# Storing some heads in pairs, with one input buffer and four output buffers, in a QK^T kernel on one core

## The chip, the core and the metric

The kernel runs on one core of a Trainium2 chip. The metric is the device time of one execution in microseconds (us); a verdict compares medians of several executions. Before the change the median of 3 runs is 1062.53 us (1062.45 to 1062.65).

A core has a matrix engine (PE) that writes to PSUM, a vector engine (DVE), a scalar engine (ACT), a GpSimd engine (POOL) and a sync engine (SP). SP and ACT issue DMA transfers here; the transfers themselves are carried out by 16 DMA engines that move data between HBM (the arrays in_q, in_k, out) and SBUF (the kernel's tiles).

## The reference

```python
def setup_inputs():
    batch, n_heads, seq, head_dim = 8, 12, 1024, 64
    ...
def reference(q, k):
    return np.einsum('bhid,bhjd->bhij', q, k).astype(np.float32)
```

There are 96 heads. For each, a 1024 x 64 matrix q is multiplied by the transpose of a 1024 x 64 matrix k, and the 1024 x 1024 float32 product is written out. Inputs are 2 x 25 MB, the output is 403 MB: 4 MB for a head.

## The kernel before

**Blocks.** The heads are taken in blocks of 2, 2, 4, 8, 8 and six times 12 (`sizes`, line 77). A block's q and k are loaded, cast to float16, and transposed so that the 64 columns lie on the partitions, before its first head can be multiplied. Blocks 0 and 1 are transposed by PE (`transpose_rows`, line 238). All later ones go through POOL, which casts 32-partition pieces into one of two half buffers (`cast_quads`, line 201, the cast on line 211), and DVE, which transposes 32 x 32 squares of a half buffer into qT or kT (`transpose_quads`, line 222, line 230). A block's q is cast and transposed in two parts, then its k in two parts (`chunks`, line 193; `CHUNK`, line 80, would cut them finer).

**One head.** `scores` (line 256) takes a head in four steps (index u, from head 1 on): PE multiplies two 128-row pieces of q with all of k into one half of PSUM (line 312), and ACT copies that half to an output buffer in SBUF (line 289, 128 x 2048 elements). When all four copies are done, SP issues one DMA that stores the head (line 302).

**Buffers.** There are three output buffers (`o_sb`, line 94), taken in a ring: the copies of a head wait until the store of the head three before it has landed (`out_free`). At the start the first output buffer holds the inputs of blocks 0 to 2 (lines 330 to 343). There are two input buffers (`x_sb`, line 88), in a ring too, one for q and one for k.

**What sets the order.** Every engine works through its own list in the order in which the Python code appends to it; semaphores alone tie the lists together. `run` and `wait` (lines 29 and 33) put a wait in front of an instruction, and nothing behind a waiting instruction on its engine goes ahead. DMA issues are entries of SP's or ACT's list.

**Loads.** The early loads and block 3's two loads are issued at the very start; store 0 also waits until block 3's q has landed (line 300). The rest form a `stream` (line 344): q and k of block 4, of block 5, and so on. `next_load` (line 350) issues the next one on ACT. `block` (line 391) calls it after the copy of step u = 1 of certain heads: heads 1 and 3 of block 2, heads 4 and 6 of blocks 3 and 4, and heads 6 and 8 of the 12-head blocks (`LOADS`, line 81; line 410). DVE's transposes for the next block, and POOL's casts, are appended along the heads of a block (lines 407 to 413).

Of the kernel before, what the change touches and what calls it, by code (L numbers as in the profile page):

```python
# [7 lines left out]
F32 = mybir.dt.float32  # L8
P = 128
# [50 lines left out]
def kernel(  # L60
# [6 lines left out]
    nc = tc.nc  # L67

    B, H, S, D = q.shape
    NT = S // P  # L70
    BH = B * H
# [2 lines left out]
    flat = [x.rearrange("b h s d -> (b h s) d") for x in (q, k)]  # L74
    of = out.rearrange("b h i j -> (b h) i j")

    sizes = [2, 2, 4, 8, 8] + [12] * ((BH - 24) // 12)
    PE_BLOCKS, EARLY = 2, 3
    NMAX = max(sizes)
    CHUNK, HALVES = 96 * 32, 2  # L80
    LOADS = {0: (), 1: (), 2: (1, 3), 3: (4, 6), 4: (4, 6)}

    pool = ctx.enter_context(tc.tile_pool(name="sb", bufs=1))
    psum = ctx.enter_context(
        tc.tile_pool(name="ps", bufs=1, space=bass.MemoryType.PSUM)
    )
    ident = pool.tile([P, P], F16, tag="ident")
    x_sb = [pool.tile([P, NMAX * S * D // P], F32, name=f"x_sb{i}", tag=f"x{i}") for i in range(2)]
    half_sb = [pool.tile([P, CHUNK], F16, name=f"half{i}", tag=f"half{i}") for i in range(HALVES)]
    qk_sb = [  # L90
        [pool.tile([P, NMAX * S // 2], F16, name=f"{'qk'[x]}T{i}") for x in range(2)]
        for i in range(2)
    ]
    o_sb = [pool.tile([P, NT, S], F32, name=f"o_sb{i}", tag=f"out{i}") for i in range(3)]
    ps_all = psum.tile([P, 4 * S], F32, tag="po")

    ctx.enter_context(tc.tile_critical())  # L97
# [2 lines left out]
    act = Engine(nc, nc.scalar, "act_done")  # L100
    dve = Engine(nc, nc.vector, "dve_done")
    gps = Engine(nc, nc.gpsimd, "pool_done")
    sp = Engine(nc, nc.sync, "sp_done")
# [18 lines left out]
    n, at = S * D // P * 2, 8 * S // 2  # L122
# [5 lines left out]
            for h in range(2)  # L128
        ]
    )  # L130
    inputs = Ring(x_sb)
    outs = Ring(o_sb)
    input_landing = {id(t): Landing(nc, f"x{i}_in") for i, t in enumerate(x_sb)}
    store_landing = {id(t): Landing(nc, f"out{i}_out") for i, t in enumerate(o_sb)}

    class Block:
        def __init__(self, i, first, N):
            self.i, self.first, self.N = i, first, N
            self.by_pe = i < PE_BLOCKS
            self.R = N * S // P  # L140
            self.elems = self.R * D
            self.cut = max(1, -(-self.R * 32 // CHUNK))
            self.raw = [None] * 2
            self.landed = [[] for _ in range(2)]
            self.raw_busy = [None] * 2
            self.rows = [None] * 2
            self.halves = {}
            self.qk = qk_sb[i % 2]
            self.ready = []
            self.over = []  # L150

        def load(self, x, eng, landing=None):
            events = []
            if self.raw[x] is None:
                buf, events, self.raw_busy[x] = inputs.next()
                self.raw[x] = buf[:, : self.elems]
                landing = input_landing[id(buf)]
            src = flat[x][self.first * S : (self.first + self.N) * S]
            eng.wait(events)
            dma = eng.eng.dma_start(  # L160
                out=self.raw[x], in_=src.rearrange("(p r) d -> p (r d)", p=P)
            )
            self.landed[x].append(landing.start(dma))
# [10 lines left out]
        def cast_rows(self, x):  # L174
            n = S * D // P
            buf, events, busy = rooms.next()
            rows = buf[:, : 2 * n].rearrange("p (r h d) -> p r h d", h=2, d=D)
            for h in range(2):
                done = gps.run(
                    lambda: nc.gpsimd.tensor_copy(  # L180
                        out=rows[:, :, h],
                        in_=self.raw[x][:, h * n : (h + 1) * n].rearrange(
                            "p (r d) -> p r d", d=D
                        ),
                    ),
                    events + [self.landed[x][h]],
                )
            self.rows[x] = rows, done, busy
            if self.raw_busy[x] is not None:
                self.raw_busy[x].append(done)  # L190
            return done

        def chunks(self):
# [7 lines left out]
        def cast_quads(self, x, part, c):  # L201
            m = self.R // self.cut
            buf, events, busy = (rooms if self.i == PE_BLOCKS else halves).next()
            dst = buf[:, : m * 32]
            raw = self.raw[x].rearrange("p (r h d) -> p r h d", h=2, d=32)
            for half in range(2):
                b = 2 * half + part
                for h in range(2):
                    q0 = 32 * (2 * half + h)
                    done = gps.run(  # L210
                        lambda: nc.gpsimd.tensor_copy(  # L211
                            out=dst[q0 : q0 + 32].rearrange("p (r d) -> p r d", d=32),
                            in_=raw[32 * b : 32 * b + 32, c * m : (c + 1) * m, h],
                        ),
                        events + self.landed[x],
                    )
            self.halves[x, part, c] = dst, done, busy
            if self.raw_busy[x] is not None:
                self.raw_busy[x][:] = [done]
            return done  # L220

        def transpose_quads(self, x, part, c):
# [33 lines left out]
        def scores(self, n, side, regions, w):  # L256
            half, g = divmod(n, self.N // 2)
            cs = slice(half * D, (half + 1) * D)
            qT = self.qk[0].rearrange("c (g m t) -> c g t m", t=NT, m=P)
            kT = self.qk[1].rearrange("c (g j) -> c g j", j=S)  # L260
            buf, out_free, out_busy = outs.next()
            written = {}
            for u in range(NT // w):
                ps, ps_free, ps_busy = regions.next()
                first = True
                for tt in range(w):
                    stationary = qT[cs, g, w * u + tt]
                    done = pe.run(
                        lambda: load_weights(stationary, half * D),
                        self.ready if n == 0 and u == 0 else [],  # L270
                        signal=False,
                    )
                    for j in range(2):
                        at = tt * S + j * 512
                        done = pe.run(
                            lambda: multiply(
                                ps[:, at : at + 512],
                                stationary,
                                kT[cs, g, j * 512 : (j + 1) * 512],
                                half * D,  # L280
                            ),
                            ps_free,
                            signal=tt == w - 1 and j == 1,
                        )
                dst = buf[:, w * u : w * u + w].rearrange("p t j -> p (t j)")
                by_dve = w == 1 and u % 2
                copier = dve if by_dve else act
                copied = copier.run(
                    lambda: (nc.vector.tensor_copy if by_dve else nc.scalar.copy)(  # L289
                        out=dst, in_=ps[:, : w * S]  # L290
                    ),
                    out_free + [done],
                )
                written[copier] = copied
                ps_busy.append(copied)
                for do in side.get(u, []):
                    do()
            self.over = [done]
            sp.wait(written.values())
            if self.first + n == 0:  # L300
                sp.wait(blocks[EARLY].landed[0])
            dma = nc.sync.dma_start(
                out=of[self.first + n].rearrange("(p t) j -> p (t j)", p=P),
                in_=buf.rearrange("p t j -> p (t j)"),
            )
            out_busy.append(store_landing[id(buf)].start(dma))

    def load_weights(stationary, at):
        return nc.tensor.ldweights(stationary, tile_position=(at, 0))  # L309
# [18 lines left out]
        first += N  # L328

    early, _, early_busy = outs.next()  # L330
    raw = early.rearrange("p t j -> p (t j)")
    at = 0
    for b in blocks[:EARLY]:
        for x in range(2):
# [15 lines left out]
    def next_load(eng):  # L350
        if stream:
            b, x = stream.pop(0)
            assert b.i == EARLY or not any(i == b.i - 1 and c[0] == x for i, c in casts)
            b.load(x, eng)

    for x in range(2):
# [34 lines left out]
    def block(i, heads, regions, w):  # L391
        b = blocks[i]
        nxt = blocks[i + 1] if i + 1 < len(blocks) else None
        for n in heads:
# [10 lines left out]
                    }  # L405
            elif nxt:
                parts = nxt.chunks()
                some = [s for m, s in enumerate(parts) if m * b.N // len(parts) == n]
                side = {0: [lambda s=s: transposed(nxt, s) for s in some]}
            if n in LOADS.get(i, (6, 8)):  # L410
                side[1] = side.get(1, []) + [lambda: next_load(act)]
            b.scores(n, side, regions, w)
            to_half(i + 2 + (n == b.N - 1))

# [15 lines left out]
    block(0, [1], halves_ps, 2)  # L430
    for i in range(1, len(blocks)):
        block(i, range(blocks[i].N), halves_ps, 2)
    sp.wait([(c, c.count) for c in store_landing.values()])


# [28 lines left out]
```

## Time and profile before

| | |
|---|---|
| median of 3 runs | 1062.53 us |
| span of the profiled execution, first to last instruction | 1060.4 us |
| PE, ACT, DVE, POOL busy | 66%, 66%, 44%, 33% of the span |
| moved by DMA | 453.19 MB: 50.33 MB read from HBM, 402.65 MB written to it |
| mean rate over the span | 427 GB/s |
| one ACT copy of 128 x 2048 | 1.86 us, four for a head |
| one head's store, issue to landing | 21.7 us (median), 4096 KB |
| one 12-head load, issue to landing | 22.0 us (median), 3072 KB |
| one transpose of 128 x 3072 by DVE, one cast of 32 x 3072 by POOL | 14.2 us, 2.5 us |
| granted TensorE clock | 1.000 |

The profiled execution is one of its own; it is not among the three that were timed. Its span leaves out what lies before the first and after the last instruction. Times of single instructions and transfers are counted from the start of the span. In the profile, q1 is the queue of the DMAs that SP issues and q10 that of those from ACT. An engine's idle time is put down to what ended it; an idle engine that nothing waits for costs nothing.

### The profile page before, as it was taken

The page shows a single profiled execution, that of the slowest core. Times are in us where ns is not written, and L with a number is a line of the kernel's source. Part 1 is how long each engine was busy: PE and PEld are TensorE (multiplying, and loading weights), DVE is VectorE, ACT ScalarE, POOL GpSimd, SP SyncE. Part 2 cuts the span into 40 slices and gives each one's busy share as a digit, 9 for nine tenths or more (in the row PEclk, how much of TensorE's full clock was granted, in tenths as well). Part 3 has the DMA queues.
Part 4 walks back from the last instruction along what each step waited for, and adds up shares of the span by engine and source line. Part 5 has one row for each costly group of instructions (what it writes and reads, how often), then busy time and mean ns, then how long its engine had stood idle before and what let it go on. Part 6 is the DMA issues. An engine that isn't in the chain of part 4 may idle for free.

```text
span 1060.4 us, 3258 instructions
## 1 busy us (share of the span) xinstructions
PE 700.5 (66%) x1568; PEld 127.3 (12%) x800; DVE 470.6 (44%) x43; ACT 697.0 (66%) x386; POOL 345.3 (33%) x158
## 2 busy tenths in 40 slices
PE   6876755765577557774577855777557777778770
PEld 2111100110111001110011100111001111111110
DVE  2998602991795006960069600795007950000000
ACT  4766755755678557775577755776557777777771
POOL 7667216436360430704307053160531600000000
DMA  9999999999999999999999999999999999999997
GB/s 376 434 435 434 432 419 430 435 428 431 433 432 428 428 435 430 430 431 423 438 431 429 433 431 434 434 429 422 426 432 435 429 434 434 434 435 430 431 434 336
DMA packets 17583, 453.19 MB, mean 427 GB/s; under 512 B 1952, under 2 KB 1952, under 8 KB 2976
## 3 DMA queue, kind: packets, MB, share of 16 engines
q1 hardware_dynamic: 14976, 410.00, 90.0%
q10 hardware_dynamic: 2592, 42.99, 9.7%
q8 instruction: 9, 0.15, 0.0%
q14 instruction: 6, 0.05, 0.0%
HBM read 50.33 MB, written 402.65 MB: 427 GB/s over the span
## 4 chain that ended last, share of the span: by engine, by line
DMA 71%; ACT 17%; PE 7%; DVE 2%; issue 1%; POOL 0%; ACTq 0%; SPq 0%
DMA out_dram<-o_sb 70%; ACT o_sb L289 17%; PE ps_all L312 7%; DVE kT L230 1%; DVE qT L230 1%; DMA o_sb<-in_q_dram 0%; PE ps_all L244 0%; POOL qT L180 0%; DVE kT L251 0%; ACT kT L251 0%; ACTq L36 0%; SPq L168 0%; SPq L459 0%; SPq L97 0%
## 5 line engine op out<-in xcount | busy, mean ns | idle before, releaser
L289 ACT COPY o_sb<-ps_all 128x2048 f32<-128x2048 f32 (+1 forms) x384 | 694.7, 1859 | 333.0 <-DMA out_dram<-o_sb 301.6
L312 PE MATMUL ps_all<-kT,qT 64*128 64x512 f16 x1536 | 696.4, 617 | 327.8 <-ACT o_sb L289 322.4
L211 POOL CAST half<-x_sb 32x3072 f16<-32x3072 f32 (+1 forms) x128 | 323.4, 2527 | 491.6 <-DMA x_sb<-in_q_dram 242.2
L230 DVE STREAM_TRANSPOSE qT<-half 128x3072 f16<-128x3072 f16 (+1 forms) x16 | 222.9, 14132 | 370.0 <-PE ps_all L312 370.0
L309 PEld LDWEIGHTS <-qT 64*128 64x128 f16 x768 | 124.2, 162 | 896.8 <-issue 889.2
L230 DVE STREAM_TRANSPOSE kT<-half 128x3072 f16<-128x3072 f16 (+1 forms) x16 | 224.2, 14217 | 2.8 <-POOL half L211 2.8
L230 DVE STREAM_TRANSPOSE kT<-kT 128x1024 f16<-128x1024 f16 x2 | 9.3, 4836 | 0.0
L230 DVE STREAM_TRANSPOSE qT<-qT 128x1024 f16<-128x1024 f16 x2 | 9.2, 4784 | 0.0
L211 POOL CAST qT<-o_sb 32x1024 f16<-32x1024 f32 x8 | 8.3, 1034 | 1.2 <-DMA o_sb<-in_q_dram 0.8
L211 POOL CAST kT<-o_sb 32x1024 f16<-32x1024 f32 x8 | 8.3, 1033 | 0.5
L251 DVE COPY qT<-ps_all 128x1024 f16<-128x1024 f16 x2 | 2.5, 1225 | 11.0 <-PE ps_all L244 11.0
L289 DVE COPY o_sb<-ps_all 128x1024 f32<-128x1024 f32 x4 | 4.9, 1225 | 4.4 <-PE ps_all L312 4.4
L244 PE MATMUL ps_all<-ident,qT 128*128 128x128 f16 x16 | 2.1, 310 | 6.7 <-POOL qT L180 6.6
L251 ACT COPY kT<-ps_all 128x1024 f16<-128x1024 f16 x1 | 1.0, 1012 | 4.7 <-PE ps_all L244 4.7
L180 POOL CAST qT<-o_sb 128x512 f16<-128x512 f32 x4 | 2.3, 612 | 3.6 <-DMA o_sb<-in_q_dram 3.6
L251 DVE COPY kT<-ps_all 128x1024 f16<-128x1024 f16 x1 | 1.2, 1225 | 4.4 <-PE ps_all L244 4.4
L251 ACT ACT_TABLE_LOAD x1 | 1.3, 1283 | 2.8 <-issue 2.8
L244 PE MATMUL ps_all<-ident,kT 128*128 128x128 f16 x16 | 2.0, 305 | 0.7 <-ACT o_sb L289 0.7
L180 POOL CAST kT<-o_sb 128x512 f16<-128x512 f32 x4 | 2.3, 613 | 0.4 <-DMA o_sb<-in_q_dram 0.4
L244 PEld LDWEIGHTS ps_all<-ident,qT 128*128 128x128 f16 x16 | 1.5, 140 | 6.9 <-POOL qT L180 6.9
L244 PEld LDWEIGHTS ps_all<-ident,kT 128*128 128x128 f16 x16 | 1.5, 136 | 3.3 <-POOL qT L211 1.6
L359 POOL MEMSET ident<- 128x128 f16 x1 | 0.2, 205 | 0.5 <-SPq L97 0.5
(5 smaller groups left out, 0.7 us busy)
## 6 DMA issues: line engine op xcount, KB each, us to landing
out_dram<-o_sb SPq DMA_DIRECT2D x96, 4096.0 KB, 21.7
x_sb<-in_q_dram ACTq DMA_DIRECT2D x6, 3072.0 KB, 22.0
x_sb<-in_k_dram ACTq DMA_DIRECT2D x6, 3072.0 KB, 21.9
x_sb<-in_q_dram SPq DMA_DIRECT2D x1, 2048.0 KB, 14.6
x_sb<-in_k_dram SPq DMA_DIRECT2D x1, 2048.0 KB, 19.6
x_sb<-in_q_dram ACTq DMA_DIRECT2D x1, 2048.0 KB, 18.3
x_sb<-in_k_dram ACTq DMA_DIRECT2D x1, 2048.0 KB, 19.1
o_sb<-in_k_dram ACTq DMA_DIRECT2D x4, 256.0 KB, 4.7
```

The lines of the kernel that those rows point to most:

```text
L180: lambda: nc.gpsimd.tensor_copy(out=rows[:, :, h], in_=self.raw[x][:, h * n : (h + 1) * n].rearrange("p (r d) -> p r d", d=D),),
L211: lambda: nc.gpsimd.tensor_copy(out=dst[q0 : q0 + 32].rearrange("p (r d) -> p r d", d=32), in_=raw[32 * b : 32 * b + 32, c * m : (c + 1) * ...
L230: lambda: nc.vector.transpose(out=dst, in_=buf.rearrange("p (r i) -> p r i", i=32)),
L244: lambda: nc.tensor.transpose(t_ps[:, t], rows[:, t], ident),
L251: lambda: copy(out=dst, in_=t_ps.rearrange("c t m -> c m t")), [done]
L289: lambda: (nc.vector.tensor_copy if by_dve else nc.scalar.copy)(out=dst, in_=ps[:, : w * S]),
L309: return nc.tensor.ldweights(stationary, tile_position=(at, 0))
L312: return nc.tensor.add_instruction(mybir.InstMatmult(name=nc.get_next_instruction_name(), ins=[nc.tensor.lower_ap(moving), nc.tensor.lower ...
L359: cleared = gps.run(lambda: nc.gpsimd.memset(ident, 0.0))
```

## The change

- A head whose number is in `PAIRS` isn't stored by itself: it is held, and the next head's store takes both in one DMA of 8 MB, out of two output buffers that lie side by side. `PAIRS` holds the third head before each load, so the pair is made of the heads 3 and 2 before the one at which a load is issued.
- A load is issued at the first step of the heads in `LOADS` (6, 10, 14, 19, then every sixth head from 24 to 78), ahead of that head's first copy, behind a wait for the landing of the store that frees its output buffer, that is of the head four before it.
- Four output buffers, all in one tile; one input buffer for q and k in turn (block 3's two lie side by side in it). A load waits for the last cast of the load before it, of whichever of q and k.
- Blocks of 2, 2, 4, 6, 10 and six times 12. Casts and transposes are cut in half (`CHUNK`): 48 rows of 32 instead of 96. `TURNS` tells at which heads they are appended.

```diff
-    sizes = [2, 2, 4, 8, 8] + [12] * ((BH - 24) // 12)
+    sizes = [2, 2, 4, 6, 10] + [12] * ((BH - 24) // 12)
...
-    CHUNK, HALVES = 96 * 32, 2
-    LOADS = {0: (), 1: (), 2: (1, 3), 3: (4, 6), 4: (4, 6)}
+    CHUNK, HALVES, OUTS = 48 * 32, 2, 4
+    TURNS = {6: (0, 0, 1, 2, 3, 3, 4, 5), 10: (1, 2, 3, 4, 6, 7, 8, 9), 12: (2, 3, 4, 5, 8, 9, 10, 11)}
+    LOADS = [6, 10, 14, 19] + [m for h in range(24, BH - 12, 12) for m in (h, h + 6)]
+    PAIRS = {m - 3 for m in LOADS}
...
-    x_sb = [pool.tile([P, NMAX * S * D // P], F32, name=f"x_sb{i}", tag=f"x{i}") for i in range(2)]
+    x_sb = pool.tile([P, NMAX * S * D // P], F32, name="x_sb", tag="x")
...
-    o_sb = [pool.tile([P, NT, S], F32, name=f"o_sb{i}", tag=f"out{i}") for i in range(3)]
+    o_sb = pool.tile([P, OUTS, NT * S], F32, name="o_sb", tag="out")
...
-    inputs = Ring(x_sb)
-    outs = Ring(o_sb)
+    input_busy = []
+    outs = Ring(list(range(OUTS)))
...
+    held = []
...
         def load(self, x, eng, landing=None):
             events = []
             if self.raw[x] is None:
-                buf, events, self.raw_busy[x] = inputs.next()
-                self.raw[x] = buf[:, : self.elems]
-                landing = input_landing[id(buf)]
+                at = x * self.elems if self.i == EARLY else 0
+                self.raw[x] = x_sb[:, at : at + self.elems]
+                landing = input_landing[x]
+                events = list(input_busy)
...
         def cast_quads(self, x, part, c):
...
-            if self.raw_busy[x] is not None:
-                self.raw_busy[x][:] = [done]
+            if self.i >= EARLY:
+                input_busy[:] = [done]
...
         def scores(self, n, side, regions, w):
...
-            buf, out_free, out_busy = outs.next()
+            i, out_free, out_busy = outs.next()
+            head = self.first + n
...
-                dst = buf[:, w * u : w * u + w].rearrange("p t j -> p (t j)")
+                dst = o_sb[:, i, w * u * S : w * (u + 1) * S]
+                if u == 0 and head in LOADS:
+                    act.wait(out_free)
+                    next_load(act)
...
+            held.append((i, out_busy))
+            if head in PAIRS:
+                return
             sp.wait(written.values())
-            if self.first + n == 0:
+            if head == 0:
                 sp.wait(blocks[EARLY].landed[0])
+            i, N = held[0][0], len(held)
             dma = nc.sync.dma_start(
-                out=of[self.first + n].rearrange("(p t) j -> p (t j)", p=P),
-                in_=buf.rearrange("p t j -> p (t j)"),
-            )
-            out_busy.append(store_landing[id(buf)].start(dma))
+                out=of[head - N + 1 : head + 1].rearrange("h (p t) j -> p h (t j)", p=P),
+                in_=o_sb[:, i : i + N],
+            )
+            stored = store_landing[i].start(dma)
+            for _, busy in held:
+                busy.append(stored)
+            held.clear()
...
-                some = [s for m, s in enumerate(parts) if m * b.N // len(parts) == n]
+                at = TURNS.get(b.N) or [m * b.N // len(parts) for m in range(len(parts))]
+                some = [s for m, s in zip(at, parts) if m == n]
                 side = {0: [lambda s=s: transposed(nxt, s) for s in some]}
-            if n in LOADS.get(i, (6, 8)):
-                side[1] = side.get(1, []) + [lambda: next_load(act)]
```

More of the change, by code (lines that the diff above doesn't have):

```diff
@@ L130 @@
     )
-    inputs = Ring(x_sb)
-    outs = Ring(o_sb)
-    input_landing = {id(t): Landing(nc, f"x{i}_in") for i, t in enumerate(x_sb)}
-    store_landing = {id(t): Landing(nc, f"out{i}_out") for i, t in enumerate(o_sb)}
+    input_busy = []
+    outs = Ring(list(range(OUTS)))
+    input_landing = [Landing(nc, f"x{i}_in") for i in range(2)]
+    store_landing = [Landing(nc, f"out{i}_out") for i in range(OUTS)]
+    held = []
     class Block:
@@ L144, in __init__ @@
             self.landed = [[] for _ in range(2)]
-            self.raw_busy = [None] * 2
             self.rows = [None] * 2
@@ L188, in cast_rows @@
             self.rows[x] = rows, done, busy
-            if self.raw_busy[x] is not None:
-                self.raw_busy[x].append(done)
             return done
@@ L217, in cast_quads @@
             self.halves[x, part, c] = dst, done, busy
-            if self.raw_busy[x] is not None:
-                self.raw_busy[x][:] = [done]
+            if self.i >= EARLY:
+                input_busy[:] = [done]
             return done
@@ L264, in scores @@
                 ps, ps_free, ps_busy = regions.next()
-                first = True
                 for tt in range(w):
@@ L330 @@
     early, _, early_busy = outs.next()
-    raw = early.rearrange("p t j -> p (t j)")
+    raw = o_sb[:, early]
     at = 0
@@ L352, in next_load @@
             b, x = stream.pop(0)
-            assert b.i == EARLY or not any(i == b.i - 1 and c[0] == x for i, c in casts)
+            earlier = (b.i, 0) if x else (b.i - 1, 1)
+            assert b.i == EARLY or not any((i, c[0]) == earlier for i, c in casts)
             b.load(x, eng)
@@ L432 @@
         block(i, range(blocks[i].N), halves_ps, 2)
-    sp.wait([(c, c.count) for c in store_landing.values()])
+    sp.wait([(c, c.count) for c in store_landing])
 _INS = ['q', 'k']
```

## The prediction, made before the changed kernel ran

> **What bounds the kernel now.** I read the page first: its 40 slices, its queues, its chain.
>
> ```profile
> DMA  9999999999999999999999999999999999999997
> GB/s 376 434 435 434 432 419 430 435 428 431 433 432 428 428 435 430 430 431 423 438 431 429 433 431 434 434 429 422 426 432 435 429 434 434 434 435 430 431 434 336
> q1 hardware_dynamic: 14976, 410.00, 90.0%
> q10 hardware_dynamic: 2592, 42.99, 9.7%
> DMA 71%; ACT 17%; PE 7%; DVE 2%; issue 1%; POOL 0%; ACTq 0%; SPq 0%
> ```
>
> The reader is to see three things. The DMA engines are never idle between the first and the last slice; the two queues fill 99.7% of 16 engines' span; and the rate hardly leaves 430 GB/s. So the kernel is bound by moving 453 MB. ACT and PE appear in the chain only because each head's copy stands between one store's landing and a later store's issue. The time can change in three ways: the DMA engines run dry, their rate changes, or the engines finish at more or less equal times.
>
> Next, the rate by stage. The windows view was asked for 17 us around each load of a 12-head block (q first, then k; columns are the window, then busy time and count for PE, PEld, DVE, ACT, POOL, then clock, DMA share, GB/s):
>
> ```profile
> 341.00:358.00 17.00, 9.55 (x22) 1.79 (x11) 0.00 (x0) 9.74 (x6) 0.00 (x0) 1.00 1.01 421
> 368.00:385.00 17.00, 9.86 (x23) 1.78 (x11) 0.00 (x0) 10.06 (x6) 13.36 (x5) 1.00 1.01 432
> 473.00:490.00 17.00, 8.65 (x20) 1.46 (x9) 0.00 (x0) 8.85 (x6) 0.00 (x0) 1.00 0.98 408
> 500.00:517.00 17.00, 9.91 (x23) 1.79 (x11) 0.00 (x0) 9.92 (x7) 13.07 (x5) 1.00 1.00 432
> 800.00:1050.00 250.00, 175.69 (x388) 31.04 (x192) 61.70 (x4) 177.80 (x98) 21.92 (x8) 1.00 1.00 433
> ```
>
> Stores alone run at 433 GB/s. The six q loads run at 416, 428, 421, 408, 426 and 418, the six k loads at 432 (one at 430). A q window loses (433 - rate)/433 x 17 us: 0.67, 0.20, 0.47, 0.98, 0.27, 0.59, together 3.2 us; the k windows lose 0.3. So all mixing of loads and stores costs 3.5 us of 1060. Then the spread: in the trace's completion records the 16 engines finish the last store between 1053.5 and 1058.9 us, mean 1055.4. The last engine ends 3.5 us behind the mean. **3.5 + 3.5 = 7.0 us is all that a better order of transfers could win.**
>
> Third, the start, from the timeline of SP, DVE and ACT:
>
> ```profile
> 37.77 0.33 SPq L302 DMA_DIRECT2D out_dram<-o_sb  x1
> 45.40 0.33 SPq L302 DMA_DIRECT2D out_dram<-o_sb  x1
> 55.87 0.33 SPq L302 DMA_DIRECT2D out_dram<-o_sb  x1
> 37.05 9.33 DVE L230 STREAM_TRANSPOSE kT<-kT 128x1024 f16<-128x1024 f16 x2
> 52.21 3.64 ACT L289 COPY o_sb<-ps_all 128x2048 f32<-128x2048 f32 x2 [0.18 <-PE ps_all L312]
> ```
>
> These are the stores of heads 2, 3 and 4. Head 4 is the first of block 2; it can't start before DVE's last transpose of that block ends at 46.4, and its last copy ends at 52.21 + 3.64 = 55.85. The DMA view, asked around each issue, gives the stores of heads 0 to 3 as issued at 18.52, 27.65, 37.77, 45.40 and landing 15.0, 15.6, 16.5 and 19.6 us later: at 33.5, 43.2, 54.3 and 65.0. One store is 9.7 us of DMA.
>
> **The change part by part.**
>
> *Heads 3 and 4 as a pair.* 6 is in LOADS, so 3 is in PAIRS: head 3 returns before its store, and SP issues one DMA for both when head 4 is written. Nothing that makes head 4 late is touched: DVE's copies and the four transposes of block 2 stand in the same order with the same waits, and PE's rows are the same in kind and order. So the issue stays at 55.87. What the DMA engines have to do until then shrinks. Block 3 has 6 heads for 8, so its q and k loads are 1536 KB each for 2048 KB: 1.05 MB less, at the 428 GB/s of the window 8 to 20 us, 2.4 us. Stores 0 to 2 follow each other without a gap (issued at 18.5, 27.65, 37.77, due at 21, 31 and 41), so they end 2.4 us sooner. Before, store 2 was due at 43.2 + 9.7 = 52.9 (15 of the engines had it at 52.8); now 50.5. Store 3 was issued at 45.40 and followed at once; now nothing is in any queue, for the first load of the stream also waits for ACT to reach head 6. From an issue to the first moving packet on idle engines: the first loads are issued at 0.90 and 0.95 and move at 2.2, so 1.3 us. The pair moves at 55.87 + 1.3 = 57.2. **The engines are dry for 57.2 - 50.5 = 6.7 us, +6.7**, and all other bytes come behind. Bounds of the delay: 0.4 (an issue is 0.33 long) to 4 us (the load issued at 337.13 moved at 341.05, though behind packets already taken up), so +5.8 to +9.4; I take 1.3, the only row with idle engines.
>
> *The dry spell lines the engines up.* At 50.3 one instruction fetch of 16 KB holds one engine for 0.97 us, which is why store 2 lands at 54.3 and not 52.9. In the spell such a delay (1.4 us) costs nothing. Whether that engine is the last at the end I can't tell: 0 to -1.4, I take **-0.7**.
>
> *Pairs at the later loads.* Fourteen pairs replace 28 stores; bytes, 32 KB packets and queue are the same, 14 completions of 9 ns per engine go (0.1 us). What changes is that a load (8 packets per engine, taken in turn with stores: 16 us for 3 MB) now lies wholly inside a 16-packet store, where before the boundary between two stores fell into its middle, 5 us after its start. In the q load at 341 us, 0.29 us was lost ahead of that boundary and 0.32 behind it. Against this, the loads are now 58 us apart, none 11 us behind the other: all would be like q loads, which come after long stretches of stores with POOL idle. Twelve or so at q's mean of 0.53 less half for the boundary: 3.2 us, against 3.5 now. Bounds: all gone, -3.5; 14 full q losses, 7.4, +3.9. I take **-0.5**, near the halves.
>
> The Trainium skill speaks to the boundary: DMA: Bandwidth & Descriptors, section "Queues, rings and completion order", says that a completion increment lands only after every earlier write of its engine, across queues. By that rule a boundary inside a load could hold up the load's packets, and pairs would win its whole share. The trace does not bear it out as a rule: the k loads hold the same boundary and run at 432.
>
> *Loads on a landing.* Already so: the copy of the head at 337.08 is released by a store's landing and ACT issues the load at 337.13.
>
> ```profile
> 337.08 1.86 ACT L289 COPY o_sb<-ps_all 128x2048 f32<-128x2048 f32 x1 [2.20 <-DMA out_dram<-o_sb]
> 337.13 0.33 ACTq L160 DMA_DIRECT2D x_sb<-in_q_dram  x1
> ```
>
> Cost 0. Queued behind the wait on ACT are that head's copies, which waited for the same landing.
>
> *One input buffer.* A load now waits for the last cast of the load before it. For head 6: transposes of 2048 take 9.4 us (18.75/2), so 1536 take 7.0; the last cast of block 3 ends near 46.4 + 2 x 7.0 + 5.9 = 66, ACT arrives at 63.5 and waits 2.5 us with head 6's copies behind it. Cover: the pair moves until 76.6 and head 5 is queued. Later, block 4's loads (2 MB ones landed after 18.3 and 19.1 us) have their last cast some 22 us after landing, 41 us after issue, and the next load comes 45 us (four heads and a load) after; 12-head loads need 22 + 26 = 48 of 56 us or more. 0.
>
> *Pairs hold a head back.* When a pair lands, ACT writes two heads (7.6 us each, 15.3), while two single stores (19.4 us) are queued. With loads four heads apart (heads 6, 10, 14) these two are the next pair: due at 19.4, there at 15.3 + 1.3: slack 2.8 us. With six apart it is larger. 0, but thin. *Halved casts and transposes* (128 POOL casts become 240 shorter ones, 32 DVE transposes 60): POOL is 33% and DVE 44% busy; 0.
>
> Sum against the profiled execution (span 1060.4, some 2.1 us outside it to the median of 1062.53): +6.7 - 0.7 - 0.5 = **+5.5, 1068.0 us**.
>
> **The rivals.** *A, not slower:* pairs end all loss in the loads, and with it the spread of the engines: 6.7 - 7.0 = -0.3, 1062.2. It decides only if all loss goes; below 1064.6 at least 4.6 of 7.0 us must go. For it: the loss sits around load starts and boundaries, and the dry spell aligns the engines. Against: part of the spread comes from nine instruction fetches of 0.9 us each on one engine, which stay. *B, worse:* every load pays q's full loss (+3.9 for -0.5), or the thin slack breaks once or twice for some 2 us: 1071 to 1073. *C, pairs write slower:* the two heads of a pair lie 4 MB apart. No row shows such a store; at the worst mixed rate, 408 for 433, the 14 pairs (117 MB) take 17 us more: 1085. The skill's same page, section "Latency and other measured facts", has copies at half rate with rows 4 MiB apart; by that figure it would be an estimated 270 us. Here only two rows are that far apart, the 8192 KB else are as before. *D, the pair is not late:* then -0.7 - 0.5, 1061.3; but head 4 would have to be written 6.7 us sooner, and no edit does that.
>
> **How the numbers follow.** The forecast, 1066 to 1070, has 0.47; A, up to 1064.6 and not faster by 2.1, 0.14, and faster still 0.03 (D, or more than the 7.0 that I found); between A and the forecast 0.14; B 0.18; C 0.04. About 0.2% (2.1 us) is what a measurement of this kernel can tell from none. So faster 0.03, same 0.14, slower 0.83. Leaving out a tenth at each end, the range is 1063.5 to 1071.5.
>
> **What would show it.** In the slices of the new profile, one hole: DMA near zero from 50 to 57 us, SP's fourth store issued at 55.9, the first load after 63.5. If stores run on through 50 us, the main step is wrong. Load windows at 433 say A, at 420 say the forecast or B. Further holes before heads 8 and 12 are stored say B; stores-only windows below 433 in pairs say C. The spread of the last store's completions, 5.4 us now, tells what lining up was worth.

## The result, and the profile after

The changed kernel takes 1075.15 us (median of 4 runs, 1074.77 to 1075.23) against 1062.59 before: 1.0119 times as long, 95% interval 1.0104 to 1.0133, 12.6 us. The prediction had the sign, but with 5.5 us less than half of it, and its range ended at 1071.5. The profiled execution has a span of 1073.4 us against 1060.4.

The page of the changed kernel, the same rows as shown of before:

```profile
DMA  9899999999999999999999999999999999999998
GB/s 391 352 371 430 427 435 433 419 430 429 426 435 423 438 421 431 432 419 441 416 425 434 421 438 410 434 429 430 429 412 436 432 419 430 430 431 431 437 430 352
q1 hardware_dynamic: 14752, 408.95, 89.4%
q10 hardware_dynamic: 2592, 44.04, 9.6%
DMA 54%; ACT 23%; PE 17%; DVE 2%; issue 1%; POOL 0%; SPq 0%; ACTq 0%
```

The reader is to see a hole in the second and third slice (352 and 371 GB/s; a slice is 26.8 us), and behind it a rate that dips to 410 to 421 in eight later slices. The queues' share fell from 99.7% to 99.0%: 0.7% of 1073 us is 7.5 us without work, and that leaves 5.5 of the span's 13.0 us to be found while the engines count as busy. The shares of the chain, last row, moved from DMA to ACT and PE (DMA has 54% for 71%); by itself that says nothing of the time, because the DMA engines are dry in one place only.

The hole, by SP's timeline and four windows (columns as in the windows of the prediction):

```profile
37.89 0.33 SPq L310 DMA_DIRECT2D out_dram<-o_sb  x1
```
```profile
55.97 0.39 SPq L310 DMA_DIRECT2D out_dram<-o_sb  x1
```
```profile
20.00:49.00 29.00, 22.77 (x63) 5.37 (x40) 23.06 (x7) 20.84 (x13) 19.88 (x16) 1.00 1.01 434
49.00:58.00 9.00, 8.43 (x19) 1.46 (x9) 9.00 (x2) 8.64 (x6) 4.00 (x3) 1.00 0.14 60
58.00:70.00 12.00, 7.77 (x18) 1.39 (x9) 12.00 (x3) 7.82 (x5) 7.70 (x6) 1.00 1.02 437
70.00:73.00 3.00, 3.00 (x8) 0.53 (x4) 3.00 (x1) 2.82 (x2) 0.00 (x0) 1.00 0.95 299
```

SP issues head 2's store at 37.89 and nothing until the pair of heads 3 and 4 at 55.97. From 49 to 58 us the DMA engines are busy for 14%, while ACT, DVE and PE work on: they are what the pair waits for. The trace also has a record of every DMA packet, with start, size and duration. These records give the ends: the engines finish head 2's store at 49.4 on average, and the pair's first packets move at 56.9, so **7.5 us dry**. The last two rows show the second loss. The pair alone moves at full rate, 437 GB/s. Then the load that ACT issued at 67.21 starts (its first packet moves at 72.2), and just before and at that start the rate falls to 299, with the engines counted as busy: packets of the store take longer.

That dip is at most of the later loads. In what follows, **loss** is the time that DMA packets took beyond the usual for their size (1213 ns for 32 KB, 912 for 24 KB), by the packet records, divided by the 16 engines. "Start" is the 4.6 us after a load's issue, "rest" the 18.4 us behind. The last column has the times at which the 16 engines completed the last store, their mean and the last of them.

| | start, all 14 loads | rest, all 14 | start, mean of the last nine | last store: mean engine, last engine |
|---|---|---|---|---|
| before | 1.3 us | 2.8 us | 0.12 us | 1055.1, 1058.6 |
| after | 7.6 | 2.9 | 0.63 | 1069.0, 1071.8 |

The loads' loss grew by 6.5 us. The mean engine ends 13.9 us later, which is 7.5 + 6.5 to within 0.1; the last engine trails the mean by 2.8 us and not 3.5, and the span grew by 13.0.

### The profile page after: what moved, and what is told of

Same layout as the page of the kernel before. It is cut to its first block, busy times and chain, and to the rows that moved or that the text cites. A ratio compares the mean times of both kernels' runs of the same rounds, so it can differ in the third digit from the quotient of the medians.

```text
span 1073.4 us, 3370 instructions
## 1 busy us (share of the span) xinstructions
PE 701.0 (65%) x1568; PEld 127.2 (12%) x800; DVE 471.1 (44%) x71; ACT 697.8 (65%) x386; POOL 366.1 (34%) x270
## 4 chain that ended last, share of the span: by engine, by line
DMA 54%; ACT 23%; PE 17%; DVE 2%; issue 1%; POOL 0%; SPq 0%; ACTq 0%
DMA out_dram<-o_sb 53%; ACT o_sb L293 23%; PE ps_all L323 17%; DVE kT L231 1%; DVE qT L231 1%; DMA o_sb<-in_q_dram 0%; PE ps_all L245 0%; POOL qT L183 0%; DVE kT L252 0%; ACT kT L252 0%; SPq L171 0%; ACTq L36 0%; SPq L470 0%; SPq L99 0%
## 5 line engine op out<-in xcount | busy, mean ns | idle before, releaser
L212 POOL CAST half<-x_sb 32x1536 f16<-32x1536 f32 (+1 forms) x240 | 344.2, 1434 | 540.4 <-DMA x_sb<-in_k_dram 235.4
L231 DVE STREAM_TRANSPOSE qT<-half 128x1536 f16<-128x1536 f16 (+1 forms) x30 | 222.7, 7704 | 216.1 <-POOL half L212 216.1
L231 DVE STREAM_TRANSPOSE kT<-half 128x1536 f16<-128x1536 f16 (+1 forms) x30 | 222.5, 7719 | 215.5 <-POOL half L212 215.5
```

Of the source, the lines that this page charges most:

```text
L212: lambda: nc.gpsimd.tensor_copy(out=dst[q0 : q0 + 32].rearrange("p (r d) -> p r d", d=32), in_=raw[32 * b : 32 * b + 32, c * m : (c + 1) * ...
L231: lambda: nc.vector.transpose(out=dst, in_=buf.rearrange("p (r i) -> p r i", i=32)),
```

## Experiments

Theory 1: the dry spell comes from the first pair alone. For the start of the loads there were three theories: P, that a load beside an 8 MB store is dear; S, that a store's issue close to the load's is dear (with pairs, the last single store is issued 0.7 us ahead of the load, against 2.2 and 5.0 us before); G, that a long stretch without reads makes the next load dear (with one input buffer all loads are six heads apart, while before, k followed two heads behind q).

**The first pair.**

```diff
-    PAIRS = {m - 3 for m in LOADS}
+    PAIRS = {m - 3 for m in LOADS[1:]}
```

> The changed kernel without the first pair: heads 3 and 4 are stored one by one, all else as changed (1075.15 us). In its trace the DMA engines are dry from 49.7 to 57.2 us. Theory (the dry spell is the pair's): it goes, and the time falls by 7.4 us to about 1067.7; the loads' loss (10.5 us of packet time, 0.6 to 1.0 us for each load) stays. Rival (the late first load of the stream and the smaller block 3 leave the engines without work anyway): still a hole near 50 us, above 1072.

Measured: 1069.87 us (ratio to before 1.0063, 1.0048 to 1.0078). The hole is gone. The DMA view of 44 to 60 us in 40 slices, after first, then this kernel:

```profile
DMA  0900900900900100000000000000000090090090
```
```profile
DMA  0930930930930930930930930950950970970990
```

(A slice of 0.4 us is shorter than a packet, and packets stand in the slice in which they start, so single slices jump; the row of zeros is the hole.) The mean engine ends at 1061.5, 7.6 us sooner than after, as the theory has it. But the last engine now trails the mean by 5.4 us, so the time falls by 5.3 and not 7.4. The same pair put by itself into a kernel without any other:

```diff
-    PAIRS = {m - 3 for m in LOADS}
+    PAIRS = {3}
```

> The changed kernel with the first pair alone (heads 3 and 4), all other heads stored one by one: the dry spell by itself. Against the one without any pair (1063.71 us): theory (the spell costs its length, less what the lining up of the engines gives back): +5 to +7 us, 1069 to 1071, with the engines' last completions closer together. Rival (the spell costs less because the loads' loss falls behind it): under +3, below 1067.

Measured: 1070.92 us (1.0071, 1.0054 to 1.0087), 7.2 us above the kernel without pairs (1063.71, next). The spell costs its length here. It did not bring the engines closer together here: the last trails by 3.8 us with it and 4.0 without.

**No pairs at all**

```diff
-    PAIRS = {m - 3 for m in LOADS}
+    PAIRS = set()
```

> The changed kernel without any pair; buffers, blocks and load times as changed. Theory P (a load started in a 16-packet store costs more): the loss falls from 0.75 us for each load to before's 0.1 to 0.5, so 1061 to 1063. Theory S (what costs is that a store is issued 0.7 us ahead of the load, against 2.2 and 5.0 before) and theory G (what costs is a long stretch without reads ahead of the load): the loss stays near 0.7 us for each, 1067 to 1068, as without the first pair alone.

Measured: 1063.71 us (1.0010, 1.0001 to 1.0019). Start loss of the last nine loads: 0.14 us each, from 0.72 with all pairs but the first. Theory P's number, 1061 to 1063, is nearly met; G falls as the reason for the dear starts, since these loads are still six heads apart. S is not yet out, because without pairs the last store is issued 2.1 us ahead of the load again.

**The pair as two DMAs**, with every wait as it was, which tells P from S:

```diff
-            dma = nc.sync.dma_start(out=..., in_=o_sb[:, i : i + N])
-            stored = store_landing[i].start(dma)
+            events = []
+            for h in range(N):
+                dma = nc.sync.dma_start(
+                    out=of[head - N + 1 + h].rearrange("(p t) j -> p (t j)", p=P),
+                    in_=o_sb[:, i + h],
+                )
+                events.append(store_landing[i + h].start(dma))
             for _, busy in held:
-                busy.append(stored)
+                busy.extend(events)
```

> The changed kernel without the first pair (1069.87 us), and each other pair stored by two DMAs of 4 MB issued one right after the other, both buffers freed by the second landing: every wait and issue as with pairs, only the DMA is cut. Theory P (the 16-packet DMA makes the start of a load dear): the loss in the 4.6 us after a late load's issue falls from 0.7 to 0.2 us, the time to 1063.5 to 1065. Theory S (the dear thing is a store issued 0.7 us ahead of the load, which pairs bring about): the loss stays 0.7 us for each, 1069 to 1070.

Measured: 1063.34 us (1.0008, 0.9998 to 1.0018), 6.5 us below the same kernel with one DMA per pair. The stores are still issued 0.6 to 0.7 us ahead of the late loads, and the start loss is 0.11 us. **P holds and S falls**: it takes the one DMA of 8 MB, and a store issued just ahead of the load isn't enough. In the two profiled executions the mean engine ends 5.6 us sooner, of which 5.0 are lost less in the starts of the 14 loads; the rest of the difference in time is the last engine, which trails by 3.2 us for 5.4. The windows view of some 5 us from a late load's issue: the loads issued at 454.2, 520.6 and 787.3 us with one DMA per pair, then those at 452.4, 518.0 and 781.8 with two:

```profile
454.00:459.00 5.00, 3.91 (x10) 0.73 (x5) 0.00 (x0) 4.25 (x3) 0.00 (x0) 1.00 0.98 370
521.00:526.00 5.00, 3.98 (x11) 0.72 (x5) 0.00 (x0) 4.80 (x3) 0.00 (x0) 1.00 1.02 378
787.00:792.00 5.00, 3.93 (x10) 0.81 (x5) 0.00 (x0) 4.16 (x3) 0.00 (x0) 1.00 1.01 364
```
```profile
452.00:457.00 5.00, 3.92 (x10) 0.82 (x5) 0.00 (x0) 4.05 (x3) 0.00 (x0) 1.00 1.05 436
518.00:523.00 5.00, 3.99 (x10) 0.65 (x4) 0.00 (x0) 4.48 (x3) 0.00 (x0) 1.00 0.92 395
782.00:787.00 5.00, 3.96 (x10) 0.66 (x4) 0.00 (x0) 4.64 (x3) 0.00 (x0) 1.00 1.02 424
```

PE, DVE, ACT and POOL do nearly the same in both; the rate differs. Over the last eight loads it is 382 GB/s in the mean against 416 (before: 425). A window this short catches whole packets or not, so the mean counts.

A pair beside a load doesn't make every start dear, though. In the changed kernel the loads at 111.3, 262.7 and 328.9 us lose 0.00, 0.23 and 0.20 us at their start with a pair moving; without the first pair those at 204.3 and 254.9 lose 0.00 and 0.04, and all nine behind them 0.50 to 0.86. What else it takes isn't shown by these runs.

**Three more against S and G.** Loads later in their head, with pairs and without:

```diff
-                if u == 0 and head in LOADS:
+                if u == NT // w - 1 and head in LOADS:
```

> The changed kernel without the first pair, its loads issued behind the third copy of their head, some 3.8 us after the landing, so 4.5 us behind the last store's issue and 4 ahead of the next. Theory S: the loss falls to at most 0.1 us for each load, the time to 1062 to 1064. Theory P: the loss stays about 0.7 us, 1069 to 1070.

> Without pairs (1063.71 us), loads behind the third copy as well: 6 us behind the last store's issue instead of 2.1. Theory S: the loss falls from 0.1 to 0.25 us for each load to under 0.1, the time by 1 to 2 us to about 1062. Theory P and theory G: no change within 1 us.

Measured: 1071.00 us (1.0078, 1.0063 to 1.0093) and 1065.47 us (1.0038, 1.0020 to 1.0056). With pairs the start loss of the last nine was 0.42 us in the mean. It grew along the run, from at most 0.45 us (0.01 to 0.45) for the first six to 0.72, 0.78 and 0.87 for the last three, although the last store's issue was some 4.4 us away from each: S fails again. Neither kernel is faster: their last engine trails the mean by 7.4 and 6.3 us, and the nine runs of the second spread from 1063.9 to 1072.3. Then the opposite, a store held back until it is issued behind the load, as `PAIRS = {m - 1 for m in LOADS[5:]}` with a store of the held head after the next head's first copy:

> Without pairs, and from head 30 on the store of the head before a load is held back until the first copy of the load's head is done: the store is issued some 2 us behind the load instead of 2.1 ahead of it. Theory S in its wide form (a store's issue within some 2 us on either side of the load's): 0.3 to 0.7 us more for each of nine loads, 1066 to 1070. Theory P: no change, 1063.7 within 1 us.

Measured: 1063.39 us (1.0007, 0.9998 to 1.0016), start loss 0.15: no change, so a store's issue 2.3 us behind the load costs nothing. And in the kernel before, `LOADS.get(i, (6, 8))` changed to `(2, 8)`:

> The kernel before, with the q load of the 12-head blocks at their head 2 instead of 6, the k load at head 8 as it was: six heads apart instead of two. Theory G (a load soon after another one is cheap): the k loads at 364 us and later lose 0.3 to 0.8 us each like the q loads, the time rises by 2 to 3 us to about 1065. Theory P (pairs): no change, 1062.6. Theory S: the k loads' distance to the store before falls from 5.0 to 2.2 us, so they lose what q loads do; here S and G agree.

Measured: 1062.91 us (1.0002, 0.9992 to 1.0011), start loss 0.12 as before, so G falls here too as far as the starts go. Over start and rest together it has something: before, the last four q loads, 104 us or so behind the load ahead of them, lose 0.6 us each and the k loads, 27 us behind, 0.1; now these eight are 66 us apart, and both kinds lose 0.4. The sum hardly changes, and so the time doesn't.

One edit missed what I meant. Loads put ahead of the third copy (`u == 2`):

> As the one without pairs, but a load is issued after the second copy of its head and not before the first, so some 3.8 us after the landing and 4.5 us after the last store's issue. Theory S (distance to the store's issue): the loss per load falls to 0.1 us or less, 1058 to 1061. Theory G (gap since the last read) and theory P: no difference to the one without pairs (within 1 us).

Measured: 1063.32 us (1.0007, 0.9998 to 1.0017), start loss 0.18. ACT issues a DMA as soon as the copy ahead of it in its list has been handed on, not when that copy is done (one load was issued at 455.12, and the two copies ahead of it in ACT's list started at 455.08 and 456.84). So most of these loads were still issued 2.2 us behind the last store, and the run says nothing about S.

**What of the 8 MB DMA does it?** Its two heads lie 4 MB apart in HBM, it has 16 packets per engine for 8, and 8 MB for 4. In these kernels the paired heads' rows go to other places, and some edges are not stored, as each expectation says. Neighbouring places for a partition's two packets:

```diff
-                out=of[head - N + 1 : head + 1].rearrange("h (p t) j -> p h (t j)", p=P),
-                in_=o_sb[:, i : i + N],
+                out=of[head - N + 1 : head + 1].rearrange("h i j -> (h i) j")
+                .rearrange("(p n t) j -> p n (t j)", p=P, n=N)[:, :, :F],
+                in_=o_sb[:, i : i + N, :F],
```

> The changed kernel without the first pair (1069.87 us); each other pair is still one DMA of 16 packets per engine, but a partition's two packets go to neighbouring places of the output and not to places 4 MB apart. Left out or changed: the rows of these pairs land in the wrong rows of the two heads, and the last 64 of each 8192 elements aren't stored (0.9 MB of 453, about 2 us less). Theory PA (the two heads 4 MB apart make loads dear): the loss at a late load's start falls from 0.7 to 0.2 us, the time to 1061 to 1063. Theory PL (it is the length, 16 packets of one DMA waiting in each engine's queue): the loss stays at 0.7 us, 1067 to 1068.

Measured: 1066.40 us (1.0036, 1.0026 to 1.0046), start loss 0.47 against 0.72. Two thirds stay, so the distance in HBM is not what makes it; whether it adds the last third, one kernel can't tell. Two DMAs of 16 packets of 16 KB:

> As the one that stores a pair by two DMAs (1063.34 us), but each of the two has 16 packets of 16 KB per engine in place of 8 of 32 KB. Changed: half of each head's elements are exchanged with the other head's, so the output is wrong in the paired heads. Smaller packets by themselves cost (611 ns for 16 KB against half of 1213) 4.5 ns x 16 x 28 = 2 us. Theory PL by count (more packets in a DMA make the load dear): 0.7 us lost at each late load, 1070 to 1072. Theory PL by bytes (8 MB in one DMA) and theory PA: 0.2 us at each, 1065 to 1066.

Measured: 1063.07 us (1.0004, 0.9995 to 1.0014), start loss 0.02. The number of packets alone doesn't do it. One DMA of 8 MB in 8 packets of 64 KB, and in 32 packets of 16 KB (both by other cuts of the same access pattern):

> The changed kernel without the first pair, each other pair one DMA of 8 MB in 8 packets of 64 KB per engine (a partition's two rows go to neighbouring places, so the rows of paired heads land in the wrong rows; all bytes are stored). By bytes (8 MB in one DMA is what makes a load's start dear): 0.4 to 0.7 us lost in the 4.6 us after a late load's issue, 1067 to 1070. By count (16 packets of a DMA in an engine's queue): 0.1 us, as with 8 packets of 32 KB, 1063 to 1064.

> As before it, but the 8 MB in one DMA of 32 packets of 16 KB per engine (rows misplaced as there, and 64 of every 4096 elements of the paired heads not stored: 1.8 MB, 4.2 us less; the smaller packets cost some 2 us more). By bytes: 0.4 to 0.7 us lost after each late load's issue, 1066 to 1068. By count: 0.7 us or more, the same. If it is the 32 KB packets of a long DMA: under 0.1 us as with 16 packets of 16 KB, 1061 to 1062.

Measured: 1095.97 us (1.0310, 1.0293 to 1.0327) and 1058.75 us (0.9965, 0.9952 to 0.9978). The start loss is 0.53 with 64 KB packets, and 0.04 with 16 KB packets in a DMA of the same 8 MB:

```profile
452.00:457.00 5.00, 3.91 (x10) 0.81 (x5) 0.00 (x0) 4.14 (x3) 0.00 (x0) 1.00 1.04 446
518.00:523.00 5.00, 3.96 (x11) 0.66 (x5) 0.00 (x0) 4.75 (x3) 0.00 (x0) 1.00 0.97 414
780.00:785.00 5.00, 3.96 (x10) 0.81 (x5) 0.00 (x0) 4.82 (x3) 0.00 (x0) 1.00 1.04 443
```

These are the same three loads in the kernel with 32 packets of 16 KB; its eight windows have a mean of 436. So it is not the bytes of the DMA either. The 1058.75 is no gain: 13 pairs leave out 1.7 MB, 3.9 us of DMA at 433 GB/s (the expectation reckoned with 14 pairs). The 1096 is no clean price for 64 KB packets: the last engine trails by up to 9.4 us, a pair's landing comes late by that, and the other engines run dry ahead of the next pair (a window from 655 to 662 us has 328 GB/s at a DMA share of 0.76). The slack that the prediction called thin breaks there.

**Other orders in the kernel before.** Loads issued by SP, in the stores' own queue (`next_load(act)` to `next_load(sp)`):

> The kernel before with its loads issued by SP, behind the store of the head before, so in one queue with the stores: no packet of a load lies beside one of a store. If what is lost comes from mixing two queues: 3.5 us of loss and part of the 3.5 us of spread go, 1057 to 1061. If it comes from every change between writing and reading: twice 0.3 to 0.6 us for each of 14 loads, as at the first store (0.6 us), 1062 to 1070. A load then lands two stores later, which the two input buffers leave room for.

Measured: 1064.89 us (1.0020, 1.0010 to 1.0029). Loads that lie beside no store of another queue still lose 3.8 us, now on their own packets. The time is in the range of the second expectation, but the loss isn't at every change between writing and reading: nothing is lost as a load begins, its last packets take up to 2.2 us for 0.91, and that befalls the six q loads of the 12-head blocks (0.28 to 0.71 us each), while the k loads close behind them lose at most 0.06. And the stores beside a load cut in two by columns:

> The kernel before, the stores that move while a load does (the two heads ahead of each load's head) cut into two DMAs of 2 MB each, 8 packets of 16 KB per engine. By bytes or by packet size: the loads' loss, 3.5 us in all, falls to 1 or less, against 28 x 72 ns = 2 us for the smaller packets: 1061 to 1062.5. By count: no gain, only the 2 us: 1064 to 1065.

Measured: 1071.81 us (1.0082, 1.0067 to 1.0097), outside every expectation. The start loss is 0.13, no better than before. The mean engine ends 4.1 us later, where 2 were expected of the smaller packets (35 heads are cut, not 28, as blocks 9 and 10 have the same heads in `LOADS`), and the last engine trails by 8.5 us. Why the engines part so far here wasn't tried. No run gave a full output faster than the kernel before.

## Why the prediction was wrong

- **The first pair: right.** Predicted 57.2 - 50.5 = 6.7 us dry, measured 56.9 - 49.4 = 7.5. The issue came at 55.97 (55.87 predicted) and the pair moved 0.9 us later (1.3 predicted; the packet times that I read before are all 0.24 us late against the instructions, so the first loads' delay was 1.0). Head 2's store ended 1.1 us sooner than I had it: 0.5 because I took 9.7 us steps from landings, which belong to the last engine (the mean engine had that store at 52.4 before and not 52.9), and 0.6 because the stores came 3.0 us sooner and not 2.4. Alone the pair costs 7.2 us; in the changed kernel, taking it out gives back 5.3.
- **Lining up, -0.7.** The last engine trails by 2.8 us after and 3.5 before, which would fit. But with the pair alone it trails by about as much as without (3.8 and 4.0), so the cause isn't shown, and that the number came out is luck as far as these runs go.
- **Pairs at the later loads: the step that failed.** I took -0.5, between -3.5 and +3.9. Measured: +6.5 in the loads, 6.2 us of time. The error was in which part of a q load's loss the pair could touch. I halved it, since half of it lay behind a boundary between stores, and the boundary would go. The rest is indeed unchanged (2.8 and 2.9 us over all loads). But what is lost ahead of the boundary, at the start, is not a property of a load: it depends on the store beside it, and grew from 0.12 us for each late load to 0.63. My windows hardly showed that part: 341:358 for a load issued at 337.13 begins 3.9 us behind the issue, and with pairs the slow packets begin 2.5 to 5 us behind it. My upper bound was the dearest kind of load in a kernel in which every store is 4 MB. No row of it shows a load beside another kind of store, so that was no bound from above.
- **The q and k loads.** That q loads cost more because they come after long stretches of stores with POOL idle was a guess, and half of it is borne out. With all loads 66 us apart, q and k lose the same, 0.4 us each over start and rest, and k loads issued close behind a q load in the stores' own queue lose next to nothing. POOL isn't the reason: in the run with loads 66 us apart it was busy beside the q loads and idle beside the k loads. What the stretch without reads does isn't known, and with it the k loads' distance to the last store's issue changed too (2.2 us for 5.0). Either way it can't make the starts dear: without pairs, loads so spaced lose 0.14 us there.
- **The rule on completions** in the Trainium skill (DMA: Bandwidth & Descriptors, section "Queues, rings and completion order") was weighed as a reason for a gain. Pairs took the completion of a store out of the middle of the loads, and the loss behind the start stayed the same: these runs show nothing for it.
- **Loads on a landing, one input buffer, thin slack: right in cost, not in every wait.** At head 6 ACT waits for the last cast, which I had as 2.5 us behind 63.5:

```profile
67.21 0.33 ACTq L163 DMA_DIRECT2D x_sb<-in_q_dram  x1
67.58 3.63 ACT L293 COPY o_sb<-ps_all 128x2048 f32<-128x2048 f32 x2 [4.01 <-POOL half L212]
```

The wait is 4.0 us, the pair covers it (58 to 70 us at 437 GB/s), and there is no second hole. At head 10, where I had no wait, ACT waits 6.7 us for a cast; that too is covered, since the stores in the queues move on at 437 GB/s from 100 to 112 us. (One transpose of 128 x 3072 takes 15.7 us and one cast of 32 x 3072 2.7 us; the 14.2 and 2.5 in the table of before are means that mix in the smaller ones.) Buffers, blocks and halved casts together, without pairs, come to +1.1 us (1.0001 to 1.0019).
- **Rivals.** A (not slower) is out. B had the sign of the missing term, at most 3.9 us for what was 6.5. C (the 4 MB distance) is out as it was put: a pair alone moves at 437, and with neighbouring places two thirds of the start loss stay. The half rate that the Trainium skill has for rows 4 MiB apart (DMA: Bandwidth & Descriptors, section "Latency and other measured facts") is seen in no run here. D (the pair is not late) is out: it was issued at 55.97.

The whole, as differences from run to run that add up by their making: 1062.6 + 1.1 (buffers and blocks) + 6.2 (later pairs: 1069.87 - 1063.71) + 5.3 (first pair, with the others there) = 1075.2 us.

**Still open** is why a load's start slows the stores beside it only for some DMAs. Over the last nine loads, stores of 8 packets of 32 KB, 16 of 16 KB and 32 of 16 KB lose 0.02 to 0.18 us, 16 of 32 KB 0.42 to 0.72, 8 of 64 KB 0.53. In these runs packets of 32 KB or more and a DMA of 8 MB had to come together; neither alone did it, and for some loads both together didn't either.

## What to carry over

Before a store is held back to be joined with a later one, add up how long the bytes in the queues will last: here nothing was issued for the 18 us ahead of the pair, what was queued lasted 11.5 of them, and the pair alone cost 7.2 us. When a kernel moves data all the time, a larger DMA needn't be free: look at the rate in the few microseconds in which another transfer starts beside it, and try the same transfer as two DMAs with the same waits. A bound taken from the old trace holds only for the kinds of transfers that the old trace has, and a window that begins behind a load's issue misses what the issue sets off.

## What the hardware showed that I had not expected

- One 8 MB store, or two of 4 MB issued together, differ by 6.5 us over 13 pairs: the store's packets slow down some 3 us after a load is issued on the other queue (up to 2.4 us for a packet of 1.21), before the load's first packet has moved (4.1 to 5 us after the issue).
- In the kernels here that never let the 16 engines run dry, the last one ends 3.2 to 8.5 us behind their mean, and the last one sets the time. In two kernels with equal start loss (0.12 us: before, and without pairs with late loads) the last engine trailed by 3.5 and 6.3 us, and the times differ by 2.9.
- An instruction fetch of 16 KB, nine in each run, takes 0.88 to 0.97 us of a single engine in the kernel before, and up to 1.5 in others.
